# Projection stage of an encoder trunk: two weight sums a group and the first heads' biases from VectorE to GpSimd, a fourth raw weight buffer, and the stores that keep x spread over the first stage

## The chip, the core and the metric

The kernel runs on one core of a Trainium2 chip. The core has a matrix engine (PE, called TensorE), VectorE (DVE), ScalarE (ACT), GpSimd (POOL) and a queue engine (SP), each with its own in-order queue of instructions; they meet only through semaphores. 16 DMA engines move data between HBM and the on-chip memory (SBUF); transfers are issued from SP, ACT or POOL. PE writes its results into PSUM banks. The metric is the device time of one execution in microseconds (us), the median of several runs.

## What is computed

Two layers of an encoder over 512 tokens of width 1024, all in float32. Cut to what matters here:

```
h = h + 0.5 * post(SwiGLU(pre(h)))            # feed-forward 1
u = pre(h);  proj = u @ w_in[l]               # 54 column blocks of 128
qa, ka, va, qb, kb, vb, qc, kc, vc, gates = split(proj)
A: neighbourhood attention, bias = rpb looked up by relative place, plus a mask
B: sliding-window attention     C: differential attention
h = h + post((sum_i gate_i * (branch_i @ W_branch_i)) @ W_out)
h = h + 0.5 * post(SwiGLU(pre(h)))            # feed-forward 2
```

Every matrix product is made with three matmuls: each operand is divided into a high part (a rounded copy, by ACT) and a low part (the rest, by DVE), and high*high, high*low and low*high are summed.

## The kernel before, in words

**Stages.** Each layer runs feed-forward 1 ("f"), the projections ("p", `project`), attention and mixing ("m", `mixer`) and feed-forward 2. In the profiled execution the projections of layer 0 lie at about 346 to 512 us and those of layer 1 at 1510 to 1668 us.

**Groups by Strassen.** In "f" and "p" most products run in groups of two column blocks with seven half-sized products instead of eight (class `Seven`, a variant of Strassen's method). One group is 84 matmuls of 128x256 on PE. "p" has 13 groups a layer, numbered g = 0 to 12 (`GROUPS`), after a few blocks that are made in the ordinary way (`COVER`). For each group DVE and ACT make the weights ready while PE works on the group before: two raw blocks of 512 KB are fetched (`fetches`, line L206), then come `sum13` (DVE, L628, 128x1024), `high1`/`low1` (ACT L632, DVE L637), `high13`/`low13` (ACT L642, DVE L647), `sum2` (DVE, L651, 128x512: writes the quarter s2 into the second raw block), `high12`/`low12` (ACT L657, DVE L661), `sum4` (DVE, L665, 128x512: after low12 has read that quarter) and `high24`/`low24` (ACT L669, DVE L674). DVE also closes each group's sums (`add21` L740, `add22` L745, which read PSUM) and, in "p", makes low parts of results (L1413), rotary products (L1459 to L1461) and transposed values (L1441, which read PSUM).

**Raw weights.** All raw blocks go through three buffers "wr", turn by turn. A fetch waits until the block that lay in its buffer has been read for the last time. So the second fetch of group g+2 goes into the buffer that holds the first block of group g+1.

**GpSimd.** In "p" POOL only issues stores of finished pieces to HBM (`store`, L1407). Each waits in POOL's queue until ACT or DVE has written its piece. In "f" it makes a one-column copy ("mark", L287) ahead of each of its transfers.

**Tiles.** Pieces of 128x512 in "p" come from a ring of 16 buffers "t"; a buffer comes free when its store has landed.

**Biases.** `mixer` adds masks to the looked-up table in four additions a head (`put`, L1750). For heads 0 and 1 the inputs are loaded in "p" (`tables_of_a`, called in group 6 of the program text, moved forward by the scheduler) and the additions run in "p" as well; for the other heads they run in "m".

**First stage.** At the start x lies transposed in SBUF. `keep(tb)` (L905 to L912) turns it back by 2 x 4 transposes of PE into the only bank "o", ACT copies each bank into a tile "h" of a ring of 4 (shared with the tiles t and v of the same stage), and SP stores it to HBM. Four `keep` calls give 8 such rounds. They are entries of a list `later`: small pieces of work that are taken up two at a time whenever a new weight tile is fetched. Ten more entries follow them (differences of the operand's quadrants and their high and low parts, and the first group's weights).

**What sets the order.** Outside two regions with an order by hand, a scheduler that lays out the whole program ahead of time decides the order on each engine's queue; on the chip each queue is then strictly in order.

Of the kernel before, what the change touches and what calls it, by code (L numbers as in the profile page):

```python
# [21 lines left out]
NT = T // P  # L22
FF = 2816
KF = FF // P
# [4 lines left out]
WB = 8  # L29
# [85 lines left out]
def encoder_kernel(ctx: ExitStack, tc: tile.TileContext, order, xT, wts, cols, rows, rpb, consts, tables, out):  # L115
    nc = tc.nc
# [8 lines left out]
    BUFS = {"X": 6, "n": 2, "wr": 3, "wp": 2, "wq": 2}  # L125
    WP = BUFS["wp"] + BUFS["wq"]
    SKEW = 80
    ABUFS = {"f": {"t": 4, "x": 10}, "p": {"t": 16, "x": 10, "rr": 2}, "m": {"t": 5, "h": 4, "rr": 2, "tx": 5, "st": 14, "gd": 2, "g": 10, "s": 2, "pt": 4}}
    PBUFS = {"mm": 2, "mx": 2, "at": 3, "o": 1}

    def open_phase(kind):
# [10 lines left out]
    def nm(s):  # L142
        serial[0] += 1
        return f"{s}{serial[0]}"
# [53 lines left out]
    def holder(tag):  # L198
        return lambda: [big(tag, F32R, (P, HB, P), name="w") for _ in range(2)]

    def fetch(parts, eng=None):
        raw = sb.tile([P, WB, P], F32, tag="wr", name=nm("wr"), bufs=BUFS["wr"])
        src = wts[len(stream["raw"])].rearrange("p (a b) -> p a b", b=P)
        for c in range(0, WB, WB // parts):
            cs = slice(c, c + WB // parts)
            (eng or stream["eng"]).dma_start(raw[:, cs, :], src[:, cs, :])  # L206
        stream["raw"].append(raw)
# [167 lines left out]
    class Squares:  # L375
        def __init__(self):
            self.acc, self.seen = None, []
# [203 lines left out]
    class Seven:  # L581


        def __init__(self, z, count):
            self.z, self.count = z, count
# [28 lines left out]
        def fetches(self, g):  # L614
            if g < self.count:
                self.W[g] = {}
                for _ in range(2):
                    fetch(1, nc.sync)
# [29 lines left out]

        def sum2(self, g):
            r = self.raws[g]  # L650
            V.tensor_tensor(out=r[1][:, 1], in0=self.W[g]["r13"][:, 1], in1=r[0][:, 0], op=ALU.add)  # L651

        def high12(self, g):
            w = self.W[g]
# [7 lines left out]

        def sum4(self, g):
            r = self.raws[g][1]
            V.tensor_tensor(out=r[:, 0], in0=r[:, 0], in1=r[:, 1], op=ALU.add)  # L665

        def high24(self, g):
            self.W[g]["h24"] = self.wpair("h24")
# [96 lines left out]
    def ffn(l, which, X, accs):  # L765
# [93 lines left out]
                V.scalar_tensor_tensor(out=place(m), in0=pu, scalar=-1.0, in1=t, op0=ALU.mult, op1=ALU.mult)  # L859


        S = Seven(z, KF - plain)
# [7 lines left out]
        def at(fn, *args):  # L870
            return lambda: fn(*args)
# [13 lines left out]
        if first:  # L885
# [33 lines left out]
            later.extend(at(keep, tb) for tb in range(NT))  # L919
            later.append(at(gap, "gaph", 48))  # L920
        else:
            quadrants(X.raw)
# [14 lines left out]
                at(S.low1, 0),  # L937
            )
        )
        if not first:  # L940
            u1 = dense1(gu, l, KF + 1, X.blocks, tag="at")
        finish(0, g0, u0)
# [427 lines left out]
    def project(l, op, accs):  # L1370
# [115 lines left out]
            now()  # L1486

        made = {}
        S = Seven(z, len(GROUPS))
        count, groups, later = S.count, S.groups, stream["later"]  # L1490

        def some(*calls):
# [226 lines left out]
    def mixer(l, op, made):  # L1719
# [15 lines left out]
        def biases(hd):  # L1735
# [10 lines left out]
            def put(dst, mask, n0, n1):  # L1746

                src = raw[:, 7 * RPBW + 39 - 8 * n0 :]
                (ps0, pn), _ = src.ap
                V.tensor_tensor(  # L1750
                    out=dst.rearrange("p (d r c) -> p d r c", r=8, c=8),
                    in0=bass.AP(src.tensor, src.offset, [[ps0, pn], [-8, n1 - n0], [-RPBW, 8], [-1, 8]]),
                    in1=mask.rearrange("p (d r c) -> p d r c", r=8, c=8),
                    op=ALU.add,
                )
# [402 lines left out]
```

## Time and profile before

| what | value |
|---|---|
| median of 3 runs | 2344.84 us (2342.85 to 2346.62) |
| profiled execution | 2345.54 us, its span 2343.7 us |
| PE busy | 2329.0 us (99% of the span) |
| DVE busy | 1917.7 us (82%) |
| ACT busy | 1455.2 us (62%) |
| POOL busy | 235.7 us (10%) |
| granted TensorE clock | 0.999 |

The span runs from the first to the last instruction; the execution's own time is 1.8 us more. "Busy" of PE is the union of its matmul records, whose ends are modelled; so what matters here is the time in which PE is not busy at all, 14.7 us of the span, and in which stage that lies.

### The profile page before, as it was taken

Reading aid. Unit: us, or ns where it says so; the run is one execution under the profiler, and the core shown is the slowest. Engines: PE = TensorE matmul, PEld = TensorE weight load, DVE = VectorE, ACT = ScalarE, POOL = GpSimd, SP = SyncE. Lnnn points to the kernel's source line nnn. Section 1 sums busy time; section 2 is a strip of 40 time slices with the busy share of each in tenths; the row PEclk is TensorE's granted clock in tenths of the full one; section 3 lists DMA queues with packets and bytes.
Section 4 is the critical chain, followed back from the end, with each engine's and each line's share of the span. In section 5 each row is a group of like instructions: output and inputs, shape, how many; then the busy total and the mean of one; then the engine's idle time right before and its main releaser. Section 6 shows DMA issues by size and latency. Waiting matters only on the chain.

```text
span 2343.7 us, 40580 instructions
## 1 busy us (share of the span) xinstructions
PE 2329.0 (99%) x15278; PEld 2104.4 (90%) x15278; DVE 1917.7 (82%) x3103; ACT 1455.2 (62%) x2734; POOL 235.7 (10%) x378
## 2 busy tenths in 40 slices
PE   9999999999999999999999999999999999999998
PEld 7999889998888889998899998899988888999987
DVE  8987988868987778888888878798689776888796
ACT  6565566668766465655665555666687764656563
POOL 0111001110122001110001100011102110011100
PEclk9999999999999999999999999999999999999999
DMA  5566446668556425665536565276775664356642
GB/s 190 148 172 194 147 150 194 200 218 241 150 179 214 149 96 151 168 160 161 171 103 165 166 171 197 92 219 197 231 221 147 187 207 142 97 162 171 180 142 92
DMA packets 135636, 395.18 MB, mean 169 GB/s; under 512 B 19216, under 2 KB 23952, under 8 KB 134928
## 3 DMA queue, kind: packets, MB, share of 16 engines
q1 hardware_dynamic: 99712, 260.11, 35.8%
q0 software_dynamic: 22080, 84.95, 13.3%
q10 hardware_dynamic: 13648, 47.53, 6.6%
q8 instruction: 120, 1.97, 0.4%
q14 instruction: 76, 0.62, 0.1%
HBM read 326.98 MB, written 80.74 MB: 174 GB/s over the span
## 4 chain that ended last, share of the span: by engine, by line
PE 88%; DMA 4%; DVE 3%; issue 2%; ACT 1%; SPq 0%; POOL 0%; ACTq 0%; DVEq 0%; POOLq 0%
PE mm L687 20%; PE mx L687 10%; PE mm L1155 8%; PE mm L323 6%; PE mm L322 6%; PE mm L324 6%; PE mx L1155 5%; PE at L687 5%; PE at L1155 5%; DMA wr<-in_wts_dram 2%; PE at L322 2%; PE at L323 2%; PE at L324 2%; PE o L1155 1%; PE mx L1677 1%
## 5 line engine op out<-in xcount | busy, mean ns | idle before, releaser
L687 PE MATMUL mm<-X,h 128*128 128x256 f32 x1600 | 285.5, 278 | 2.3 <-DVE v L745 2.2
L687 PEld LDWEIGHTS mm<-X,h 128*128 128x128 f32 x1600 | 243.1, 188 | 4.3 <-DVE v L745 3.4
L687 PE MATMUL mm<-ht,h 128*128 128x256 f32 x800 | 224.0, 280 | 1.0 <-ACT at L726 1.0
L687 PE MATMUL mm<-ht,l 128*128 128x256 f32 x800 | 223.6, 279 | 0.0
L687 PE MATMUL mm<-lt,h 128*128 128x256 f32 x800 | 222.8, 278 | 0.0
L687 PE MATMUL mx<-ht,h 128*128 128x256 f32 x800 | 221.6, 277 | 0.4 <-ACT v L731 0.2
L687 PE MATMUL mm<-X,l 128*128 128x256 f32 x800 | 221.5, 277 | 0.0
L687 PE MATMUL mx<-ht,l 128*128 128x256 f32 x800 | 221.2, 276 | 0.0
L687 PE MATMUL mx<-lt,h 128*128 128x256 f32 x800 | 221.2, 276 | 0.0
L219 ACT ACTIVATE w<-wr 128x512 fp32r<-128x512 f32 x240 | 148.1, 626 | 96.4 <-PE mm L324 54.7
L220 DVE TENSOR_TENSOR w<-wr,w 128x512 fp32r<-128x512 f32 x240 | 163.0, 687 | 49.6 <-ACT w L219 48.6
L322 PE MATMUL mm<-X,w 128*128 128x512 f32 (+1 forms) x516 | 196.3, 380 | 0.3 <-ACT w L219 0.3
L323 PE MATMUL mm<-X,w 128*128 128x512 f32 (+1 forms) x516 | 195.4, 379 | 0.2
L324 PE MATMUL mm<-X,w 128*128 128x512 f32 (+1 forms) x516 | 193.6, 375 | 0.0
L637 DVE TENSOR_TENSOR l<-wr,h 128x1024 fp32r<-128x1024 f32 x100 | 122.4, 1224 | 67.8 <-PE mm L687 67.6
L669 ACT ACTIVATE h<-wr 128x1024 fp32r<-128x1024 f32 x100 | 106.2, 1062 | 84.1 <-PE mx L687 56.1
L687 PE MATMUL at<-X,w 128*128 128x256 f32 x1200 | 153.7, 277 | 0.0
L687 PEld LDWEIGHTS mm<-ht,h 128*128 128x128 f32 x800 | 150.7, 188 | 1.6 <-ACT at L726 1.4
L687 PEld LDWEIGHTS mx<-ht,h 128*128 128x128 f32 x800 | 150.3, 188 | 1.1 <-ACT v L731 1.0
L687 PEld LDWEIGHTS mm<-ht,l 128*128 128x128 f32 x800 | 150.8, 188 | 0.3 <-DVE l L674 0.2
L687 PEld LDWEIGHTS mm<-lt,h 128*128 128x128 f32 x800 | 150.7, 188 | 0.0
L687 PEld LDWEIGHTS mx<-lt,h 128*128 128x128 f32 x800 | 150.3, 188 | 0.0
(462 smaller groups left out, 6767.0 us busy)
## 6 DMA issues: line engine op xcount, KB each, us to landing
wr<-in_wts_dram SPq DMA_DIRECT2D x284, 512.0 KB, 3.7
wr<-in_wts_dram ACTq DMA_DIRECT2D x90, 512.0 KB, 4.2
sum<-in_wts_dram POOLq DMA_DIRECT2D x64, 512.0 KB, 5.1
st<-part SPq DMA_DIRECT2D x120, 128.0 KB, 4.2
ap<-in_wts_dram SPq DMA_DIRECT2D x20, 512.0 KB, 6.0
a<-kept SPq DMA_DIRECT2D x32, 256.0 KB, 6.3
ap<-sum SPq DMA_DIRECT2D x16, 512.0 KB, 3.3
x<-part SPq DMA_DIRECT2D x32, 256.0 KB, 3.6
```

The costliest lines, as they stand in the source:

```text
L219: A.activation(hi, raw, AF.Copy)
L220: V.tensor_tensor(out=lo, in0=raw, in1=f(hi), op=ALU.subtract)
L322: PE.matmul(acc, w[0], x[0], start=start, stop=False)
L323: PE.matmul(acc, w[0], x[1], start=False, stop=False)
L324: PE.matmul(acc, w[1], x[0], start=False, stop=stop)
L637: V.tensor_tensor(out=w["l1"], in0=self.raws[g][0], in1=f(w["h1"]), op=ALU.subtract)
L669: A.activation(self.W[g]["h24"], self.raws[g][1], AF.Copy)
L687: PE.matmul(acc, ws[i], xs[j], start=start and k == m == 0, stop=stop and k == n - 1 and m == 2, skip_group_check=True,)
L1155: PE.matmul(acc, x[i], w[j], start=start and n == 0, stop=stop and n == 2, skip_group_check=True)
L1677: PE.matmul(shaped(sp, k), qs, k, start=m == 0, stop=m == 1)
```

## The change

Four edits, three of them in "p":

- `sum2` and `sum4` of groups 2 to 12 are issued on GpSimd (`self.adder`), those of groups 0 and 1 stay on VectorE; the class is also used in "f", where the adder stays VectorE. That is 22 additions of 128x512 a layer.
- The four `put` additions of heads 0 and 1 are issued on GpSimd: 8 a layer, four of 128x256 and four of 128x128.
- In "p" the second raw block of every odd group goes to a buffer of its own, "wx". So there are four raw buffers for two groups, and a fetch for group g+2 waits for group g alone. The room comes from the ring "t", which has 14 buffers now.
- The four `keep` entries are no longer in one row ahead of the other ten: they stand before the first, second, third and fourth of these.

```
--- before.py
+++ after.py
@@ -125,7 +125,7 @@
     BUFS = {"X": 6, "n": 2, "wr": 3, "wp": 2, "wq": 2}
     WP = BUFS["wp"] + BUFS["wq"]
     SKEW = 80
-    ABUFS = {"f": {"t": 4, "x": 10}, "p": {"t": 16, "x": 10, "rr": 2}, "m": {"t": 5, "h": 4, "rr": 2, "tx": 5, "st": 14, "gd": 2, "g": 10, "s": 2, "pt": 4}}
+    ABUFS = {"f": {"t": 4, "x": 10}, "p": {"t": 14, "x": 10, "rr": 2}, "m": {"t": 5, "h": 4, "rr": 2, "tx": 5, "st": 14, "gd": 2, "g": 10, "s": 2, "pt": 4}}
     PBUFS = {"mm": 2, "mx": 2, "at": 3, "o": 1}
 
     def open_phase(kind):
@@ -198,8 +198,9 @@
     def holder(tag):
         return lambda: [big(tag, F32R, (P, HB, P), name="w") for _ in range(2)]
 
-    def fetch(parts, eng=None):
-        raw = sb.tile([P, WB, P], F32, tag="wr", name=nm("wr"), bufs=BUFS["wr"])
+    def fetch(parts, eng=None, raw=None):
+        if raw is None:
+            raw = sb.tile([P, WB, P], F32, tag="wr", name=nm("wr"), bufs=BUFS["wr"])
         src = wts[len(stream["raw"])].rearrange("p (a b) -> p a b", b=P)
         for c in range(0, WB, WB // parts):
             cs = slice(c, c + WB // parts)
@@ -581,8 +582,8 @@
     class Seven:
 
 
-        def __init__(self, z, count):
-            self.z, self.count = z, count
+        def __init__(self, z, count, adder):
+            self.z, self.count, self.adder = z, count, adder
             self.hi, self.lo, self.raw = {}, {}, {}
             self.raws, self.W = {}, {}
             self.groups = [{} for _ in range(count)]
@@ -614,8 +615,9 @@
         def fetches(self, g):
             if g < self.count:
                 self.W[g] = {}
-                for _ in range(2):
-                    fetch(1, nc.sync)
+                for i in range(2):
+                    own = phase[0][0] == "p" and i and g % 2
+                    fetch(1, nc.sync, self.z("wx", F32, (P, WB, P)) if own else None)
                 self.raws[g] = [t.rearrange("p (a b) c -> p a b c", a=2) for t in stream["raw"][-2:]]
 
         def wpair(self, name):
@@ -648,7 +650,7 @@
 
         def sum2(self, g):
             r = self.raws[g]
-            V.tensor_tensor(out=r[1][:, 1], in0=self.W[g]["r13"][:, 1], in1=r[0][:, 0], op=ALU.add)
+            (self.adder if g > 1 else V).tensor_tensor(out=r[1][:, 1], in0=self.W[g]["r13"][:, 1], in1=r[0][:, 0], op=ALU.add)
 
         def high12(self, g):
             w = self.W[g]
@@ -662,7 +664,7 @@
 
         def sum4(self, g):
             r = self.raws[g][1]
-            V.tensor_tensor(out=r[:, 0], in0=r[:, 0], in1=r[:, 1], op=ALU.add)
+            (self.adder if g > 1 else V).tensor_tensor(out=r[:, 0], in0=r[:, 0], in1=r[:, 1], op=ALU.add)
 
         def high24(self, g):
             self.W[g]["h24"] = self.wpair("h24")
@@ -859,7 +861,7 @@
                 V.scalar_tensor_tensor(out=place(m), in0=pu, scalar=-1.0, in1=t, op0=ALU.mult, op1=ALU.mult)
 
 
-        S = Seven(z, KF - plain)
+        S = Seven(z, KF - plain, V)
         hi, lo, raw, groups, count = S.hi, S.lo, S.raw, S.groups, S.count
         divide, less, quadrants = S.divide, S.less, S.quadrants
         later = stream["later"]
@@ -916,7 +918,6 @@
                 later.append(some(at(normal, b), at(normal, b + 1)))
             later.append(at(divide, "11", own[0][:, 0], own[1][:, 0]))
             later.append(at(divide, "22", own[0][:, 1], own[1][:, 1]))
-            later.extend(at(keep, tb) for tb in range(NT))
             later.append(at(gap, "gaph", 48))
         else:
             quadrants(X.raw)
@@ -937,6 +938,9 @@
                 at(S.low1, 0),
             )
         )
+        if first:
+            for tb in range(NT):
+                later.insert(len(later) - 10 + tb, at(keep, tb))
         if not first:
             u1 = dense1(gu, l, KF + 1, X.blocks, tag="at")
         finish(0, g0, u0)
@@ -1486,7 +1490,7 @@
             now()
 
         made = {}
-        S = Seven(z, len(GROUPS))
+        S = Seven(z, len(GROUPS), G)
         count, groups, later = S.count, S.groups, stream["later"]
 
         def some(*calls):
@@ -1747,7 +1751,7 @@
 
                 src = raw[:, 7 * RPBW + 39 - 8 * n0 :]
                 (ps0, pn), _ = src.ap
-                V.tensor_tensor(
+                (G if hd < 2 else V).tensor_tensor(
                     out=dst.rearrange("p (d r c) -> p d r c", r=8, c=8),
                     in0=bass.AP(src.tensor, src.offset, [[ps0, pn], [-8, n1 - n0], [-RPBW, 8], [-1, 8]]),
                     in1=mask.rearrange("p (d r c) -> p d r c", r=8, c=8),
```

**DVE, layer 0, group 7 of "p" while the weights of group 8 (r_5254, wr_5206 and wr_5208) are made ready.** Before:

```order
L628 TENSOR_TENSOR r_5254<-wr_5208,wr_5206 128x1024
L661 TENSOR_TENSOR w_5290<-wr_5208,w_5290 128x512
L637 TENSOR_TENSOR l_5270<-wr_5206,h_5251 128x1024
L651 TENSOR_TENSOR wr_5208<-r_5254,wr_5206 128x512
L647 TENSOR_TENSOR l_5307<-r_5254,h_5268 128x1024
L740 TENSOR_TENSOR v_5272<-mx_5235,v_5272 128x256
L665 TENSOR_TENSOR wr_5208<-wr_5208 128x512
L1413 TENSOR_TENSOR lo_5360<-x_4931,hi_5359 128x512
L745 TENSOR_TENSOR v_5272<-mm_5234,v_5272 128x256
L674 TENSOR_TENSOR l_5382<-wr_5208,h_5355 128x1024
```

and now (line numbers are two higher in this part, L1413 is L1417):

```order
L630 TENSOR_TENSOR r_5254<-wx_5208,wr_5206 128x1024
L742 TENSOR_TENSOR v_5139<-mx_5102,v_5139 128x256
L1465 TENSOR_TENSOR v_4862<-v_4862,sh_5018 128x512
L676 TENSOR_TENSOR l_5249<-wr_5069,h_5222 128x1024
L1417 TENSOR_TENSOR lo_5226<-v_4725,hi_5225 128x512
L747 TENSOR_TENSOR v_5139<-mm_5101,v_5139 128x256
L663 TENSOR_TENSOR w_5290<-wx_5208,w_5290 128x512
L630 TENSOR_TENSOR r_5387<-wr_5341,wr_5339 128x1024
L639 TENSOR_TENSOR l_5270<-wr_5206,h_5251 128x1024
L649 TENSOR_TENSOR l_5307<-r_5254,h_5268 128x1024
L742 TENSOR_TENSOR v_5272<-mx_5235,v_5272 128x256
L676 TENSOR_TENSOR l_5382<-wx_5208,h_5355 128x1024
```

`sum2` and `sum4` are gone from DVE's queue, and `sum13` of a group now stands ahead of the closing sums v_5139 and of the low part l_5249 of the group before, where it stood behind them; even sum13 of the group after (r_5387) stands ahead of low1 (l_5270).

**POOL, layer 0, the start of the groups** (edges and pre are the biases' outputs and inputs, wr_4224 and r_4263 belong to group 2). Now:

```order
L1411 DMA part_4099<-v_4092 128x512
L1754 ISA
L1754 TENSOR_TENSOR edges_5100<-pre_5095 128x256
L653 TENSOR_TENSOR wr_4224<-r_4263,wr_4222 128x512
L1754 TENSOR_TENSOR edges_5100<-pre_5095 128x128 x2
L1754 TENSOR_TENSOR edges_5100<-pre_5095 128x256 x2
L1754 TENSOR_TENSOR edges_5100<-pre_5095 128x128
L667 TENSOR_TENSOR wr_4224<-wr_4224 128x512
L1411 DMA part_4301<-hi_4297 128x512
L1411 DMA part_4303<-lo_4298 128x512
L653 TENSOR_TENSOR wx_4365<-r_4409,wr_4363 128x512
```

Before, the store of part_4301 came right behind that of part_4099. The row "ISA" reloads POOL's library of routines; it stands there once, and not in layer 1. Between the two sums of group 2 stand bias additions (one more of 128x256 is left out here), and between later sums stand stores that wait for ACT and DVE.

**ACT, the copies h of the first stage** (o is the bank, h the tile of the ring of 4 that is stored). Before:

```order
L910 ACTIVATE h_471<-o_466 128x512
L206 DMA wr_611<-in_wts_dram 128x1024
L854 ACTIVATE t_486<-t_486 128x512
L910 ACTIVATE h_504<-o_499 128x512
L219 ACTIVATE w_564<-wr_562 128x512
L910 ACTIVATE h_512<-o_507 128x512
L600 ACTIVATE ht_567<-n_358 128x1024
L910 ACTIVATE h_521<-o_516 128x512
```

and now:

```order
L912 ACTIVATE h_455<-o_450 128x512
L601 ACTIVATE X_359<-n_358 128x1024
L220 ACTIVATE w_512<-wr_477 128x512
L207 DMA wr_611<-in_wts_dram 128x1024
L856 ACTIVATE t_470<-t_470 128x512
L912 ACTIVATE h_489<-o_484 128x512
L220 ACTIVATE w_551<-wr_549 128x512
L601 ACTIVATE ht_515<-n_358 128x1024
L912 ACTIVATE h_497<-o_492 128x512
```

Before, four copies had been made by h_471 and a further two follow the tiles t and v of the ring; now two copies stand ahead of t and v (h_455 is the second), and the next two come with more work between them.

More of the change, by code (lines that the diff above doesn't have):

```diff
@@ L127, in encoder_kernel @@
     SKEW = 80
-    ABUFS = {"f": {"t": 4, "x": 10}, "p": {"t": 16, "x": 10, "rr": 2}, "m": {"t": 5, "h": 4, "rr": 2, "tx": 5, "st": 14, "gd": 2, "g": 10, "s": 2, "pt": 4}}
+    ABUFS = {"f": {"t": 4, "x": 10}, "p": {"t": 14, "x": 10, "rr": 2}, "m": {"t": 5, "h": 4, "rr": 2, "tx": 5, "st": 14, "gd": 2, "g": 10, "s": 2, "pt": 4}}
     PBUFS = {"mm": 2, "mx": 2, "at": 3, "o": 1}
@@ L199, in holder, with fetch @@
         return lambda: [big(tag, F32R, (P, HB, P), name="w") for _ in range(2)]
-    def fetch(parts, eng=None):
-        raw = sb.tile([P, WB, P], F32, tag="wr", name=nm("wr"), bufs=BUFS["wr"])
+    def fetch(parts, eng=None, raw=None):
+        if raw is None:
+            raw = sb.tile([P, WB, P], F32, tag="wr", name=nm("wr"), bufs=BUFS["wr"])
         src = wts[len(stream["raw"])].rearrange("p (a b) -> p a b", b=P)
@@ L581, in encoder_kernel, with __init__ @@
     class Seven:
-        def __init__(self, z, count):
-            self.z, self.count = z, count
+        def __init__(self, z, count, adder):
+            self.z, self.count, self.adder = z, count, adder
             self.hi, self.lo, self.raw = {}, {}, {}
@@ L616, in fetches @@
                 self.W[g] = {}
-                for _ in range(2):
-                    fetch(1, nc.sync)
+                for i in range(2):
+                    own = phase[0][0] == "p" and i and g % 2
+                    fetch(1, nc.sync, self.z("wx", F32, (P, WB, P)) if own else None)
                 self.raws[g] = [t.rearrange("p (a b) c -> p a b c", a=2) for t in stream["raw"][-2:]]
@@ L650, in sum2 @@
             r = self.raws[g]
-            V.tensor_tensor(out=r[1][:, 1], in0=self.W[g]["r13"][:, 1], in1=r[0][:, 0], op=ALU.add)
+            (self.adder if g > 1 else V).tensor_tensor(out=r[1][:, 1], in0=self.W[g]["r13"][:, 1], in1=r[0][:, 0], op=ALU.add)
         def high12(self, g):
@@ L664, in sum4 @@
             r = self.raws[g][1]
-            V.tensor_tensor(out=r[:, 0], in0=r[:, 0], in1=r[:, 1], op=ALU.add)
+            (self.adder if g > 1 else V).tensor_tensor(out=r[:, 0], in0=r[:, 0], in1=r[:, 1], op=ALU.add)
         def high24(self, g):
@@ L859, in finish @@
                 V.scalar_tensor_tensor(out=place(m), in0=pu, scalar=-1.0, in1=t, op0=ALU.mult, op1=ALU.mult)
-        S = Seven(z, KF - plain)
+        S = Seven(z, KF - plain, V)
         hi, lo, raw, groups, count = S.hi, S.lo, S.raw, S.groups, S.count
@@ L918, in ffn @@
             later.append(at(divide, "22", own[0][:, 1], own[1][:, 1]))
-            later.extend(at(keep, tb) for tb in range(NT))
             later.append(at(gap, "gaph", 48))
@@ L939, in ffn @@
         )
+        if first:
+            for tb in range(NT):
+                later.insert(len(later) - 10 + tb, at(keep, tb))
         if not first:
@@ L1488, in project @@
         made = {}
-        S = Seven(z, len(GROUPS))
+        S = Seven(z, len(GROUPS), G)
         count, groups, later = S.count, S.groups, stream["later"]
@@ L1749, in put @@
                 (ps0, pn), _ = src.ap
-                V.tensor_tensor(
+                (G if hd < 2 else V).tensor_tensor(
                     out=dst.rearrange("p (d r c) -> p d r c", r=8, c=8),
```

## The prediction

> **What bounds the kernel now.** I read first where PE, the busiest engine, is not busy, stage by stage, in the view of busy time by stretch (length; then busy us and instruction count of PE, weight loads, DVE, ACT, POOL; clock; DMA share; GB/s).
>
> ```profile
> 0.00:72.00 72.00, 69.09 (x337) 57.84 (x337) 59.94 (x106) 46.34 (x78) 2.14 (x8) 1.00 0.51 169
> 72.00:223.00 151.00, 151.00 (x1321) 150.81 (x1321) 128.64 (x163) 87.65 (x145) 24.87 (x30) 1.00 0.62 167
> 346.00:512.00 166.00, 164.27 (x1339) 159.80 (x1338) 140.45 (x196) 106.69 (x199) 24.85 (x46) 1.00 0.62 196
> 1510.00:1668.00 158.00, 156.00 (x1255) 150.81 (x1254) 136.38 (x187) 100.97 (x188) 22.73 (x42) 1.00 0.64 198
> 2214.00:2343.70 129.70, 123.50 (x597) 102.81 (x595) 97.56 (x113) 64.71 (x92) 0.00 (x0) 0.99 0.41 133
> ```
>
> PE is the bound. The change adds and removes no matmul, so it can win only the time in which PE waits where the change works: part of 2.91 us in the first stage, 1.73 us in the projections of layer 0 and 2.00 us in those of layer 1. The 6.2 us at the end are out of its reach. What it can lose has no such bound: where DVE's work in the projections gets longer than PE's, DVE becomes the clock. So I read next who made PE wait, in the view of waits cut to three stretches: 36 to 62 us (one row), 391 to 502 (three) and 1552 to 1665 (two); us, times, longest.
>
> ```profile
> PE o L908 <- ACT h L910: 1.6, 1, 1.6
> ...
> PE at L1434 <- DVE v L1441: 0.8, 1, 0.8
> PE mm L687 <- DVE v L745: 0.7, 2, 0.5
> PE mx L687 <- ACT v L731: 0.2, 1, 0.2
> ...
> PE mm L687 <- ACT at L726: 1.0, 1, 1.0
> PE mm L687 <- DVE v L745: 0.6, 2, 0.4
> ```
>
> These are few and short waits. In the projections most are for DVE, which was late with a sum or a transposed value.
>
> **The stores of x (first stage).** One wait of 1.6 us. Its cause is ahead of ACT:
>
> ```profile
> 49.53 0.60 ACT L910 ACTIVATE h<-o 128x512 f32<-128x512 f32 x1 [2.78 <-DMA kept<-h]
> DMA to landing us min/median/max: 2.0/4.0/5.6
> ```
>
> The first row is ACT's timeline, the second the landing times of the eight stores at L911. The sixth copy waited 2.78 us for its tile h, since a store from the ring of four had not landed, and PE's next transposes waited for the one bank. In the new order a copy's tile was last used by tiles t and v, which have no store, or by a store with at least 23 matmuls and two other copies in between, where before four copies stood in a row and the sixth met the fourth's store. I take it that even a store of 5.6 us has landed by then. What it can cost: three of the four last rounds stand close together, and a copy of 0.60 us may show between them. So the bounds are -1.6 and +0.6 us; I take **-1.3 us**, near the wait that is seen, since its cause is removed and the spacing of the later rounds is like that of the early rounds of before, which did not wait.
>
> **What leaves DVE.** The two rows of the sums in the groups by line between 391 and 502 us, with the rows that read PSUM, and the bias additions of the whole run (ns, min/median/max):
>
> ```profile
> L665 DVE TENSOR_TENSOR wr<-wr 128x512 f32<-128x512 f32 x11 | 7.6, 687 | 0.1
> L651 DVE TENSOR_TENSOR wr<-r,wr 128x512 f32<-128x512 f32 x11 | 7.5, 684 | 0.0
> L740 DVE TENSOR_TENSOR v<-mx,v 128x256 f32<-128x256 f32 x11 | 4.6, 421 | 0.9 <-PE mx L687 0.9
> L745 DVE TENSOR_TENSOR v<-mm,v 128x256 f32<-128x256 f32 x11 | 4.6, 419 | 0.0
> L1441 DVE TENSOR_TENSOR v<-at,v 128x256 fp32r<-128x256 f32 x6 | 2.5, 420 | 0.0
> L1750 DVE TENSOR_TENSOR edges<-pre x16: 282/353/421, 390.2 to 1575.6; 128x256 f32<-128x256 f32 x8, 128x128 f32<-128x128 f32 x8
> ```
>
> ```profile
> 391.00:502.00 111.00, 109.27 (x942) 108.18 (x941) 99.62 (x138) 72.79 (x139) 20.46 (x38) 1.00 0.65 207
> 1552.00:1665.00 113.00, 111.04 (x947) 109.46 (x947) 100.26 (x139) 73.56 (x140) 20.48 (x38) 1.00 0.64 204
> ```
>
> Sums 7.6 + 7.5 = 15.1 us and eight additions of 0.35 us = 2.8 us a layer leave DVE: 99.6 becomes about 81.7 of 111 us, and 100.3 becomes 82.4 of 113.
>
> **What it costs on POOL.** The trace has no addition on POOL. Below, a sum costs what DVE takes for it, 0.69 us. Above, I add POOL's dearest small instruction, the one-column copy:
>
> ```profile
> L287 POOL COPY mark<-a x53: 757/1046/1047, 93.9 to 2199.5; 128x1 f32<-128x1 f32 x53
> 93.66 1.22 DVE L647 TENSOR_TENSOR l<-r,h 128x1024 fp32r<-128x1024 f32 x1
> 93.88 1.03 POOL L287 COPY mark<-a 128x1 f32<-128x1 f32 x1 [8.12 <-DVE a L982]
> 94.79 0.42 DVE L740 TENSOR_TENSOR v<-mx,v 128x256 f32<-128x256 f32 x1
> ```
>
> 1.05 + 0.69 = 1.74 us. I take the middle, 1.2 us, and for a bias addition the share of its size (256 or 128 of 512 columns, on average 0.375), 0.45 us. That is 22 x 1.2 + 8 x 0.45 = 30 us a layer. POOL was busy 20.5 of 111 us, so the work fits in its queue.
>
> The rows show something else. A copy of one column that lasts 1.03 us and ends at 94.91 does not work that long: L647, which reads two SBUF operands, ends at 94.88. So POOL got at its operand when DVE's instruction let go. I assume the same the other way: while POOL adds, a DVE instruction with two SBUF operands waits. DVE's idle time (111 - 81.7 = 29.3 us) and the rows that read PSUM (4.6 + 4.6 + 2.5 = 11.7 us) are free of that; the other 70 us, 63% of the stretch, are not. If POOL's 30 us fall without regard to DVE, 0.63 x 30 = 19 us are added to DVE: 81.7 + 19 = 101 of 111 us, against 99.6 before. **So I count no relief of DVE at all.** With 0.69 us a sum it would be 92.6 us, with 1.74 us for a sum and 1.4 us for a bias 113 us.
>
> [...]
>
> **The fourth raw buffer.** What DVE and ACT waited for between 391 and 502 us (two rows), DVE between 1552 and 1665 (one), and what the fetches in SP's queue waited for between 391 and 502 (last):
>
> ```profile
> DVE r L628 <- DMA wr<-in_wts_dram: 4.8, 8, 0.9
> ...
> ACT w L657 <- DMA wr<-in_wts_dram: 9.5, 8, 3.2
> ...
> DVE r L628 <- DMA wr<-in_wts_dram: 2.7, 5, 1.2
> ...
> SPq L206 <- DVE l L637: 26.5, 5, 7.4
> ```
>
> DVE stood still 4.8 and 2.7 us for raw blocks that came late, and the fetches were late because the buffer still held the first block of the next group until low1 (L637) had read it. With "wx" a fetch no longer waits for that, and the new order has sum13 a third of a group earlier. Those stops of DVE go, and with them some of PE's waits behind them (the closing sum L745 stands in the order close to L628). The earlier sum13 also covers the longer way of the two sums over POOL. All of PE's waits in both stages are 1.73 + 2.00 = 3.7 us; one of 1.0 us is ACT's, and the others need not all come from the raw blocks. I take half, **-1.9 us**; the bounds are -3.7 and the rivals below.
>
> **The smaller ring "t".** No cost: a store lands 4.5 us (at most 6.5) after its issue in the view by line, and 14 buffers are two groups of work. If POOL's queue delays stores, that cover shrinks.
>
> ```profile
> DMA to landing us min/median/max: 2.2/4.5/6.5
> ```
>
> **Sum.** -1.3 - 1.9 = -3.2 us on the profiled execution of 2345.54 us (span 2343.7 and 1.8 us around it): 2342.3. That execution lies 0.7 us above the median of the runs, 2344.84, so the prediction is **2341.6 us** for the median, -0.14%. A change below 0.2%, 4.7 us, can hardly be told from none for this kernel.
>
> **Rivals.**
>
> *All waits go.* The exclusion touches little, since POOL's sums come early and find gaps. Then -1.6 - 3.7 = -5.3 us: 2339.5. For it: DVE's queue is 18 us shorter in each stage. Against: one of PE's longest waits there is ACT's.
>
> *POOL's queue is late at the first groups.* In layer 0 POOL reloads its library and makes seven bias additions ahead of sum4 of group 2. POOL's row before:
>
> ```profile
> 384.69 0.54 POOL L1407 DMA_DIRECT2D part<-v  x1 [1.53 <-DVE v L1441]
> 395.81 0.54 POOL L1407 DMA_DIRECT2D part<-hi  x1 [10.58 <-ACT v L735]
> 398.42 0.68 DVE L665 TENSOR_TENSOR wr<-wr 128x512 f32<-128x512 f32 x1
> ```
>
> POOL is free from 385.2 us; before, sum4 of group 2 ended on DVE at 399.1, 13.9 us later. Two sums and seven additions are 5.6 us, and if each of the nine waits half of a DVE instruction of 1.22 us, 5.5 us more: 11.1 us. A reload over 2.8 us makes sum4 late, and DVE's low24, the sums behind it and PE with it. The stores of the next pieces then queue behind it as well. [...]
>
> *DVE becomes the bound.* Slower: a sum holds the port for 1.4 us, and nearly every one lands on a DVE instruction with two SBUF operands, since these are queued without gaps. Then DVE needs 81.7 + 22 x 1.4 + 8 x 0.525 = 116.7 of 111 us and 82.4 + 35 = 117.4 of 113: +5.7 + 4.4 - 1.3 = +8.8, 2353.6. It decides from 81.7 + 25 p = 111, a price p of 1.17 us that is wholly on top. Against it: 41 us of DVE's time there are free of the exclusion.
>
> **How the numbers follow.** Forecast 47% (own range 2340 to 2344), all waits go 20%, POOL late at the start 17%, DVE the bound 16%. Faster by over 0.2% (under 2340.2): the second case and a little of the first, 0.24. Slower by over 0.2% (over 2349.5): the last case and the dear end of the third, 0.18. Within: 0.58. The range reaches from 2337.5, two us under the second case for waits that the records do not show as idle time, to 2350, where the last case begins: it leaves out about 2 in 10.
>
> **What would show it.** In the new profile: the wait of PE for h (L912) is gone from the first 72 us; DVE's waits for "wr" or "wx" are gone; PE's idle time between 391 and 502 us is near 0.9 us instead of 1.73; POOL's additions last about 1.2 us, or up to 1.2 us longer when they start beside a DVE addition, and DVE's additions beside them have longer records or start late. I am wrong if DVE's busy time in that stretch comes out well under 95 us (then the exclusion is small), if it fills the stretch and PE's waits for DVE grow, or if PE shows a new wait of some us near 400 us.

## The result

The changed kernel takes 2382.11 us (2376.48 to 2387.12), the kernel before 2344.84 us: the ratio is 1.0158 [1.0146, 1.0171], 37 us slower. The profiled execution has a span of 2380.5 us against 2343.7, 36.8 us more. Two single executions among the experiments, 4704.5 us with the fourth buffer and 3876.7 us with `sum2` alone on POOL, lie far outside the rest and are left out of the ratios and of the second kernel's median (the first one's, 2347.74, would be 2347.47).

Busy time by stretch of the kernel after (length; busy us and count of PE, weight loads, DVE, ACT, POOL; clock; DMA share; GB/s), then the first row of its page:

```profile
0.00:72.00 72.00, 70.18 (x353) 59.19 (x354) 61.79 (x109) 47.16 (x80) 2.14 (x8) 1.00 0.54 177
391.00:502.00 111.00, 97.30 (x776) 95.94 (x775) 85.14 (x95) 62.86 (x119) 56.50 (x60) 0.92 0.54 176
```

```profile
PE 2339.8 (98%) x15278; PEld 2114.9 (89%) x15278; DVE 1911.4 (80%) x3043; ACT 1458.8 (61%) x2734; POOL 322.9 (14%) x438
```

The first stage gained: PE is busy 1.1 us more in the first 72 us. The loss is in the projections. Between 391 and 502 us PE stands 13.7 us where it stood 1.7, and it did not meet its old pace while it ran: the granted clock is 0.92. Over the whole span PE's idle time is 2380.5 - 2339.8 = 40.7 us against 14.7 (+26.0), and its busy time grew by 10.8 us although it runs the same 15278 matmuls. Here are the stretches in which the clock was granted by half, one after each of PE's longest stalls:

```profile
403.59:410.41 6.82, 4.79 (x22) 4.79 (x23) 5.17 (x7) 4.32 (x10) 4.01 (x6) 0.50 0.69 240
451.37:458.20 6.83, 6.23 (x29) 6.23 (x30) 6.44 (x9) 1.67 (x4) 0.00 (x0) 0.50 0.18 52
...
sum 30.71, PE 24.61 PEld 24.62 DVE 24.15 ACT 16.79 POOL 12.43; mean PE 4.10 PEld 4.10 DVE 4.02 ACT 2.80 POOL 2.07
```

The sum goes over six such stretches, three in each layer; the kernel before has none in its projections.

Who made PE wait (whole span; us, times, longest), and what DVE waited for at `sum13` (now L630) between 391 and 502 us:

```profile
PE mm L689 <- DVE v L747: 17.4, 8, 4.7
PE at L1438 <- DVE lo L1417: 7.6, 2, 4.1
```

```profile
DVE r L630 <- DMA wx<-in_wts_dram: 11.4, 3, 4.6
DVE r L630 <- issue: 5.1, 2, 2.6
...
DVE r L630 <- DMA wr<-in_wts_dram: 2.1, 2, 1.7
```

PE waits for DVE's closing sums (L747) and low parts (L1417). DVE does not fill the stretch: it is busy for 85.1 us of 111 and gets through 95 instructions where it made 138. It is late: 18.6 us of the stretch it stands at `sum13` for a raw block, against 4.8 before, with all that is queued behind. ("issue" is a wait without a releaser in the records; both times `sum13` reads a pair "wr" that was fetched shortly before.)

The exclusion between the two engines can be seen directly. DVE and POOL in layer 0, then lines of the whole run (ns, min/median/max):

```profile
442.64 1.23 DVE L630 TENSOR_TENSOR r<-wx,wr 128x1024 f32<-128x1024 f32 x1 [4.57 <-DMA wx<-in_wts_dram]
443.78 1.22 DVE L639 TENSOR_TENSOR l<-wr,h 128x1024 fp32r<-128x1024 f32 x1
443.95 2.21 POOL L653 TENSOR_TENSOR wx<-r,wr 128x512 f32<-128x512 f32 x1 [4.77 <-DVE r L630]
444.92 2.32 DVE L649 TENSOR_TENSOR l<-r,h 128x1024 fp32r<-128x1024 f32 x1
447.16 0.41 DVE L742 TENSOR_TENSOR v<-mx,v 128x256 f32<-128x256 f32 x1
```

```profile
L667 POOL TENSOR_TENSOR wx<-wx x10: 1277/1295/1578, 407.2 to 1676.4; 128x512 f32<-128x512 f32 x10
L1754 POOL TENSOR_TENSOR edges<-pre x16: 446/1290/1717, 387.1 to 1577.2; 128x256 f32<-128x256 f32 x8, 128x128 f32<-128x128 f32 x8
L649 DVE TENSOR_TENSOR l<-r,h x100: 1211/1220/2322, 63.4 to 2245.7; 128x1024 fp32r<-128x1024 f32 x100
L747 DVE TENSOR_TENSOR v<-mm,v x100: 408/418/425, 75.5 to 2257.7; 128x256 f32<-128x256 f32 x100
```

`sum2` is released by the end of `sum13` (L630) and begins beside L639, which reads two SBUF operands. It lasts 2.21 us, 0.93 longer than the 1.28 of an undisturbed sum, until about when L639 lets go plus 1.28. L649, begun at 444.92, lasts 1.1 us too long and ends 1.1 us after the sum. Here they take turns, each for a whole instruction. L747, which reads PSUM and one SBUF operand, is never lengthened (at most 425 ns in 100).

### The profile page after: what moved, and what is told of

It is laid out like the page before. It is cut to its first block, busy times and chain, and to the rows that moved or that the text cites. A ratio compares the mean times of both kernels' runs of the same rounds, so it can differ in the third digit from the quotient of the medians.

```text
span 2380.5 us, 40656 instructions
## 1 busy us (share of the span) xinstructions
PE 2339.8 (98%) x15278; PEld 2114.9 (89%) x15278; DVE 1911.4 (80%) x3043; ACT 1458.8 (61%) x2734; POOL 322.9 (14%) x438
## 5 line engine op out<-in xcount | busy, mean ns | idle before, releaser
L689 PE MATMUL mm<-X,h 128*128 128x256 f32 x1600 | 292.0, 282 | 17.4 <-DVE v L747 17.4
L689 PEld LDWEIGHTS mm<-X,h 128*128 128x128 f32 x1600 | 247.9, 192 | 20.0 <-DVE v L747 19.4
L639 DVE TENSOR_TENSOR l<-wr,h 128x1024 fp32r<-128x1024 f32 x100 | 123.4, 1234 | 73.4 <-PE mm L689 73.4
L689 PEld LDWEIGHTS mm<-X,l 128*128 128x128 f32 x800 | 153.3, 192 | 0.0
```

What stands on the lines that cost most here:

```text
L639: V.tensor_tensor(out=w["l1"], in0=self.raws[g][0], in1=f(w["h1"]), op=ALU.subtract)
L689: PE.matmul(acc, ws[i], xs[j], start=start and k == m == 0, stop=stop and k == n - 1 and m == 2, skip_group_check=True,)
```

## The experiments

The theories, as the expectations name them. **A**: DVE and POOL shut each other out of SBUF while POOL adds. **B**: the bias additions in POOL's queue make the sums late. **C**: the raw buffer, the ring and the order that came with them cost. **D**: the way over POOL makes the ring "load, sum13, sum2, sum4, low24, next load" longer, and DVE stands at `sum13`. Line numbers shift by a few where an experiment adds lines: `sum13` is L630 or L634.

The parts of the change together. The three columns at the right are read in 391 to 502 us: PE busy, DVE busy and DVE's waits for raw blocks at `sum13`. A slower kernel does less of its work in that stretch.

| kernel | us | ratio to before | PE | DVE | waits |
|---|---|---|---|---|---|
| before | 2344.84 | | 109.3 | 99.6 | 4.8 |
| stores of x alone | 2343.61 | 0.9992 [0.9983, 1.0001] | 109.8 | 100.2 | 2.6 |
| + fourth raw buffer, ring 14 | 2347.74 | 1.0012 [1.0002, 1.0022] | 107.9 | 98.1 | 8.7 |
| + buffer, biases on POOL | 2350.64 | 1.0025 [1.0016, 1.0033] | 105.5 | 96.4 | 11.7 |
| + buffer, sums on POOL | 2371.21 | 1.0108 [1.0094, 1.0122] | 98.9 | 87.9 | 16.8 |
| all (the change) | 2382.11 | 1.0158 [1.0146, 1.0171] | 97.3 | 85.1 | 18.6 |

### The change in parts

The first run is the kernel before with this alone:

```
-            later.extend(at(keep, tb) for tb in range(NT))
...
+        if first:
+            for tb in range(NT):
+                later.insert(len(later) - 10 + tb, at(keep, tb))
```

> The kernel before with the one edit of the stores that keep x. All theories of the loss are about the projections, so all expect the 1.6 us wait of PE for h in the first stage to go and nothing else to move: -1.3 us against before (bounds -1.6 and +0.6), about 2343.5 us, PE busy about 70.2 of the first 72 us instead of 69.1. A loss of more than 1 us would say that some of the 37 us come from here.

It measured 2343.61 us, 1.2 less than the runs of before beside it (2344.77), though the interval touches 1. As forecast.

The others start from the change and take parts back:

```
-        S = Seven(z, len(GROUPS), G)
+        S = Seven(z, len(GROUPS), V)
...
-                (G if hd < 2 else V).tensor_tensor(
+                V.tensor_tensor(
```

Both hunks together leave the stores and the fourth buffer:

> The changed kernel with the sums and the bias additions back on VectorE: what stays is the moved stores of x, the fourth raw buffer and the ring t of 14. Theory A (VectorE and GpSimd keep each other from SBUF while GpSimd adds) and theory B (GpSimd's queue: the sums stand behind bias additions and come late) both expect no loss: 2341 to 2344 us, VectorE's waits for the raw blocks (4.8 and 2.7 us in the two layers) gone, the granted clock 1.0 throughout. Theory C (the loss comes from the buffer, the smaller ring or the order of the block loads that these bring) expects PE stalls of 3 to 5 us in the projections and at least 2355 us.

2347.74 us: 4.1 us slower than the stores alone. No theory had this: not the 2355 us or more of C, and not the gain of A, B and of the prediction. DVE's waits for raw blocks did not go. Its waits and its order in this kernel:

```profile
DVE r L630 <- DMA wx<-in_wts_dram: 5.9, 3, 3.4
DVE r L630 <- DMA wr<-in_wts_dram: 2.8, 2, 2.0
```

```profile
428.05 1.22 DVE L676 TENSOR_TENSOR l<-wx,h 128x1024 fp32r<-128x1024 f32 x1
429.19 0.69 DVE L663 TENSOR_TENSOR w<-wr,w 128x512 fp32r<-128x512 f32 x1
429.79 0.42 DVE L747 TENSOR_TENSOR v<-mm,v 128x256 f32<-128x256 f32 x1
430.12 0.68 DVE L667 TENSOR_TENSOR wr<-wr 128x512 f32<-128x512 f32 x1
434.23 1.23 DVE L630 TENSOR_TENSOR r<-wx,wr 128x1024 f32<-128x1024 f32 x1 [3.42 <-DMA wx<-in_wts_dram]
```

```profile
429.29 0.33 SPq L207 DMA_DIRECT2D wx<-in_wts_dram  x1
```

L676, `low24` of group 5, is the last reader of "wx". 20 ns after its end the fetch for group 7 is issued, and `sum13` of group 7 (L630) stands only three short instructions later in DVE's queue. The load takes till 434.2. So the buffer still binds, and the new order puts `sum13` ahead of work that could have filled the time. This order is not the sums' doing: without the sums' own rows, DVE's order here differs from that of the change in a few places only.

The sums alone and the biases alone, one hunk each:

> The changed kernel with only the bias additions back on VectorE; the 22 sums a layer stay on GpSimd. Theory B expects the first and longest stall of each layer (4.8 us at 400.7, 4.7 us at 1582.2) to go, with its stretch of half clock (6.8 us, worth 3.4): 8.2 us a layer, so about 2382 - 16 = 2366 us or less, and if the later stalls are its aftermath, near 2345. Theory A expects the later stalls (448.8, 492.0, 1629.8, 1671.8) to stay as they are and the first to shrink only by the queueing: 2366 to 2382 us, with VectorE instructions of 2 us and more beside GpSimd's sums.

> The changed kernel with the sums back on VectorE; only the eight bias additions of the first two heads in each layer are on GpSimd. Theory A expects little: 8 x 1.3 = 10 us of GpSimd a layer against VectorE, once, near the start of the stage: 0 to +3 us on the result of the kernel with the sums and the biases both on VectorE, no stall at 448 or 1630 us. Theory B without the sums behind the additions expects no loss either, since then only the edges themselves are late: 2341 to 2345 us. A loss of 8 us or more would say that the bias additions alone make VectorE late, whatever the sums do.

2371.21 and 2350.64 us. The sums cost 23.5 us on top of 2347.74, the biases 2.9 (the two intervals in the table overlap), and together they cost 34.4, 8.0 more than one by one. The early stall of PE, 4.7 us up to 405.6 in the change, is 1.9 us up to 401.5 with the sums alone; the later ones, near 445 and 487 us in this run, stay. So the sums are where A had them and B had not, the biases alone are in A's range of 0 to +3 and not where B had them, and B may hold for the 8 us. The whole: -1.2 + 4.1 + 23.5 + 2.9 + 8.0 = 37.3 us.

### Reads without a chain, and a chain without reads

From here on the biases are on VectorE unless the text says otherwise. First, 22 additions a layer whose results nobody waits for, beside sums on VectorE (the ring t has 13 buffers here, for the room of the tile that they write):

```
+        def beside(self, g, a, b):
+            if phase[0][0] == "p" and g > 1:
+                G.tensor_tensor(out=self.dm, in0=a, in1=b, op=ALU.add)
...
             V.tensor_tensor(out=r[1][:, 1], ...)
+            self.beside(g, r[1][:, 1], r[1][:, 1])
...
             V.tensor_tensor(out=r[:, 0], ...)
+            self.beside(g, r[:, 0], r[:, 1])
```

> The kernel with moved stores, fourth raw buffer and sums and biases on VectorE (2347.7 us), and beside it 22 additions of 128x512 a layer on GpSimd that read two finished blocks and write a tile that nobody reads (ring t 13 for its room): GpSimd's reads without VectorE, ScalarE or PE waiting for their results. VectorE's and PE's order is the same as without them. Theory A (VectorE and GpSimd shut each other out of SBUF) expects most of the 23.5 us that the sums on GpSimd cost: at least +12, 2360 us or more, with VectorE instructions of over 2 us beside them. Theory D (the way over GpSimd makes the ring load - sum13 - sum2 - sum4 - low24 - next load longer, VectorE stands at sum13 for the raw block, and what is behind it is late) expects at most +4: 2347 to 2352 us.

2375.77 us, ratio 1.0126 [1.0109, 1.0143]: 28.0 us of loss from additions whose results are not used. DVE's order is that of the row "+ fourth raw buffer, ring 14" of the table. The first rows of the pages of that run, of the sums on POOL, and of this one:

```profile
PE 2326.5 (99%) x15278; PEld 2103.0 (90%) x15278; DVE 1915.5 (82%) x3103; ACT 1458.6 (62%) x2734; POOL 236.2 (10%) x378
```

```profile
PE 2334.9 (99%) x15278; PEld 2110.2 (89%) x15278; DVE 1915.0 (81%) x3059; ACT 1458.7 (62%) x2734; POOL 314.4 (13%) x422
```

```profile
PE 2337.2 (98%) x15278; PEld 2111.3 (89%) x15278; DVE 1945.3 (82%) x3103; ACT 1457.3 (61%) x2734; POOL 315.7 (13%) x422
```

44 additions made the same 3103 DVE instructions longer by 29.8 us, 14.9 a layer. With the real sums on POOL, DVE lost 44 sums (44 x 0.686 = 30.2 us) and its busy time is 1915.0 against 1915.5: what left came back as holds. In 391 to 502 us DVE is busy 100.5 and waits 7.1 at `sum13`, 107.6 of 111, while PE did 97.4 us of work: here DVE is the clock. (The reads also hold blocks a little longer, but the waits at `sum13` are not above the 8.7 us of the kernel without them.) But DVE still makes the 44 sums here, so the holds come on top of a full queue, where in the change they take the place of the sums. The run shows that reads alone can cost this much, not how the 23.5 us come about.

The counterpart keeps the chain and takes away the reads; each sum on POOL is replaced by two writes, so the sums of groups 2 to 12 are left out of the output:

```
+        def write(self, t):
+            for _ in range(2):
+                G.memset(t, 0.01)
```

> The kernel with the sums on GpSimd and the biases on VectorE (2371.2 us), where each of the 44 sums is two writes of a constant into the same place: same waits and the same order of VectorE and PE, but GpSimd reads nothing (the output leaves out these sums). Theory D expects the loss to stay if a pair of writes lasts about as long as an addition (1.3 us): 2363 to 2373 us, VectorE's waits at sum13 still over 14 us a layer. Theory A expects the result of the sums on VectorE: 2345 to 2352 us.

2346.56 us, ratio 1.0004 [0.9994, 1.0013]. Its groups by line (first row), waits and stretch:

```profile
L628 POOL MEMSET wr<- 128x512 f32 x48 | 25.4, 530 | 51.5 <-DVE r L634 32.0 <-DMA wr<-in_wts_dram 13.7 <-DVE w L667 4.8
```

```profile
DVE r L634 <- DMA wx<-in_wts_dram: 10.1, 3, 4.3
DVE r L634 <- issue: 4.6, 2, 2.3
DVE r L634 <- DMA wr<-in_wts_dram: 3.5, 2, 1.9
```

```profile
391.00:502.00 111.00, 109.64 (x948) 108.83 (x948) 84.32 (x116) 73.04 (x139) 42.19 (x80) 1.00 0.63 209
```

A pair of writes is 1.06 us, 0.2 less than an addition, in the same place of the same order. DVE waits 18.2 us at `sum13`, as much as in the change, and PE loses nothing: DVE is relieved (84.3 us), comes early, and waits in time it has to spare. So D alone is refuted as the cause, and the waits at `sum13` alone are no loss. Without POOL's reads, taking the sums from DVE would have cost nothing, and gained nothing that shows: the 1.2 us below 2347.74 are within the noise. The writes are neither held off (530 and 532 ns on average, 48 and 40 of them) nor do they hold DVE (`low1`, 100 of 128x1024, lasts 1223 ns on average here as in the run without sums on POOL, and 1241 ns beside the 44 reads); how the 23.5 us divide between these two sides of the exclusion no run separates.

So in this pair of runs DVE and POOL were in each other's way where POOL read SBUF (28.0 us, DVE's instructions 29.8 us longer) and not where it only wrote (-1.2 us). VectorE's side, which the trace of before could not show, is in L649 (up to 2.32 us for 1.22) and L747 (at most 425 ns) above.

### More raw buffers, fewer sums

A fifth buffer, first with the sums on POOL, then with all on VectorE (the edit is the same, ring t 12):

```
-                    fetch(1, nc.sync, self.z("wx", F32, (P, WB, P)) if own else None)
+                    fetch(1, nc.sync, self.z(f"wx{g // 2 % 2}", F32, (P, WB, P)) if own else None)
```

> The kernel with the sums on GpSimd and the biases on VectorE (2371.2 us), with a fifth raw buffer: the second blocks of the odd groups take turns in two buffers, ring t 12. Theory D expects the loads for the odd groups' second blocks to come a whole group pair earlier, VectorE's wait at sum13 (16.5 and 16.8 us a layer) to fall by more than half, and the time by 10 us or more: 2350 to 2361 us. Theory A expects 2366 to 2372 us, since GpSimd reads as much as before.

> The kernel with sums and biases on VectorE (2347.7 us) with the same fifth raw buffer and ring t 12: the cost of the smaller ring without the sums. If the 4 us that the fourth buffer lost against the kernel with the moved stores alone (2343.6) are VectorE's waits for the raw block at sum13 (8.7 us in 391 to 502), they go: 2341 to 2345 us. If the smaller ring t costs, it is 2348 us or more.

2361.32 us, ratio 1.0066 [1.0051, 1.0081], and 2341.58 us, ratio 0.9984 [0.9974, 0.9993]. The waits for a load at `sum13` fell from 16.8 to 7.9 us and from 8.7 to 3.4:

```profile
DVE r L630 <- DMA wr<-in_wts_dram: 3.4, 3, 1.4
```

With them went 9.9 us beside the sums on POOL, and 6.2 us with the sums on VectorE. Read with the run of writes, this says that the waits at `sum13` count where DVE has little time to spare. The sums' own cost hardly went with them: between these two kernels it is 19.7 us, where it was 23.5. The second of these kernels is faster than both the kernel before and the change (3.3 us less than before; against the stores alone, 2343.61 in another run, the 2 us are not settled). It needs none of GpSimd's additions.

Another division of five buffers, three for all first blocks and two for all second ones, sums on VectorE:

```
-                    own = phase[0][0] == "p" and i and g % 2
+                    own = phase[0][0] == "p" and i
...
+                    fetch(1, nc.sync, self.z(f"wx{g % 2}", F32, (P, WB, P)) if own else None)
```

> The kernel with moved stores, sums and biases on VectorE and five raw buffers (2341.6 us when the second blocks of the odd groups have two), now with three buffers for the first blocks and two for the second blocks of all groups. If VectorE's waits for raw blocks are all that the fifth buffer took away, it is the same within 2 us: 2340 to 2344 us. If a buffer's turn still decides, the even division shows less waiting at sum13 (3.4 us in 391 to 502 with the other division) and 2338 to 2341 us.

2348.30 us, ratio 1.0016 [1.0007, 1.0025], with 9.6 us of waits at `sum13`, all for "wx". Neither expectation held. So the number of buffers alone does not decide; that it is how early the next one comes free fits the waits, but no run tests it by itself.

Three buffers, as before, with the sums on POOL (`own = False`, ring t 16):

> The kernel with the sums on GpSimd and the biases on VectorE (2371.2 us) without the fourth raw buffer, ring t 16: the moved stores and the sums alone, in an order of VectorE that is nearly that of the kernel before. If the sums cost the same 23.5 us wherever the buffers are, it is 2343.6 + 23.5 = 2367 us. If the order that came with the fourth buffer (sum13 ahead of the low parts that free the buffer) is a partner in the loss, VectorE waits for raw blocks well under 16.5 us in 391 to 502, and it is 2350 to 2360 us. If the fourth buffer took waits away from the sums, as the prediction had it, it is 2372 us or more with longer waits at sum13.

2361.02 us, ratio 1.0059 [1.0042, 1.0076], 17.4 us over the stores alone; a microsecond above the range for a partner. So the fourth buffer costs 10.2 us beside sums on POOL and 4.1 without them, but the sums by themselves, with 2.6 us of waits at `sum13`, cost 17.4: with three, four and five buffers 17.4, 23.5 and 19.7 us. Where these come from is seen in POOL, DVE and ACT of this kernel:

```profile
403.24 4.94 POOL L653 TENSOR_TENSOR wr<-r,wr 128x512 f32<-128x512 f32 x1 [0.26 <-DVE r L630]
...
406.95 0.41 DVE L742 TENSOR_TENSOR v<-mx,v 128x256 f32<-128x256 f32 x1
408.26 1.29 POOL L667 TENSOR_TENSOR wr<-wr 128x512 f32<-128x512 f32 x1
...
409.58 1.06 ACT L671 ACTIVATE h<-wr 128x1024 fp32r<-128x1024 f32 x1 [3.33 <-POOL wr L667]
...
410.68 1.23 DVE L676 TENSOR_TENSOR l<-wr,h 128x1024 fp32r<-128x1024 f32 x1 [3.31 <-ACT h L671]
```

This is the exclusion from the other side: DVE's instructions with two SBUF operands followed each other without a gap until L742, which reads PSUM, and `sum2` took 4.94 us. `sum4`, high24 on ACT and low24 on DVE came late one after the other, DVE stood 3.31 us, and PE 1.85 us behind it.

Half of the sums:

```
-            (self.adder if g > 1 else V).tensor_tensor(out=r[:, 0], in0=r[:, 0], in1=r[:, 1], op=ALU.add)
+            V.tensor_tensor(out=r[:, 0], in0=r[:, 0], in1=r[:, 1], op=ALU.add)
```

and the same with sum2 in place of sum4.

> The kernel with the sums on GpSimd and the biases on VectorE (2371.2 us), with sum4 back on VectorE: only sum2 on GpSimd, released by the end of sum13, so that it always starts on VectorE's next instructions. Theory A says that every hold on the burst of VectorE's work behind a late sum13 is paid: with half the holds, 8 to 14 us of the 23.5 stay: 2356 to 2362 us. If the loss has a threshold (VectorE full only with all of them), it is 2348 to 2354 us.

> The same with sum2 back on VectorE: only sum4 on GpSimd, which follows low12 and is followed by ScalarE's high24 and VectorE's low24. Theory A: 2356 to 2362 us, as with sum2 alone. If it is the longer way to low24, which frees the raw block, that costs, sum4 alone costs more than sum2 alone: 2362 us or more against 2354 or less.

2365.86 us, ratio 1.0094 [1.0075, 1.0112], and 2364.81 us, 1.0083 [1.0070, 1.0097]: 18.1 and 17.1 us over 2347.74. Both miss A's range and that of a threshold, and `sum4` alone is not dearer than `sum2` alone, as the longer way to low24 would have it: half of the sums cost nearly what all cost. With sum4 alone on POOL one sum in each layer took 7.43 us:

```profile
L667 POOL TENSOR_TENSOR wr<-wr x12: 1287/1460/7432, 392.5 to 1671.4; 128x512 f32<-128x512 f32 x12
```

Part of it is that the other sum is again DVE's. DVE's busy time, less the sums that left it, grew by 21.2 us with `sum2` on POOL (1921.6 us in all), 10.0 with `sum4` (1910.4) and 29.7 with both (1915.0): the holds add up, the time does not. Why it saturates so early is not settled: the clock is at half for 10.2 us in each of the two kernels and for 17.1 us with all sums, and DVE's orders differ a little; no run separates these.

The queue of POOL at the start of the groups, in the change with its biases on POOL:

```
-            (self.adder if g > 1 else V).tensor_tensor(
+            (self.adder if g > 3 else V).tensor_tensor(
```

(in both sums)

> The changed kernel with the sums of groups 2 and 3 back on VectorE; the sums of groups 4 to 12 and the eight bias additions a layer stay on GpSimd. Theory B (the bias additions stand in GpSimd's queue ahead of sum4 of group 2, so the first stall of a layer comes) expects the stalls at 400.7 and 1582 us (4.8 and 4.7 us) and the half clock behind them to go: the sums' 23.5 us by 18/22 are 19.2, and with the biases' own 2.9 us on 2347.7 it is 2369.8: 2366 to 2373 us. If the biases and the sums add up to 34.4 us for another reason (GpSimd's reads alone), 4 sums fewer are worth some 5 us: 2375 to 2379 us.

2370.73 us, ratio 1.0109 [1.0095, 1.0122], as B had it. What went is this, POOL and DVE in the change:

```profile
390.09 1.29 POOL L653 TENSOR_TENSOR wr<-r,wr 128x512 f32<-128x512 f32 x1 [1.69 <-DMA pre<-in_rpb_dram]
391.34 8.20 POOL L1754 TENSOR_TENSOR edges<-pre 128x256 f32<-128x256 f32 x6
399.51 1.28 POOL L667 TENSOR_TENSOR wr<-wr 128x512 f32<-128x512 f32 x1
```

```profile
401.91 2.72 DVE L676 TENSOR_TENSOR l<-wr,h 128x1024 fp32r<-128x1024 f32 x1 [2.35 <-ACT h L671]
404.56 0.68 DVE L1417 TENSOR_TENSOR lo<-x,hi 128x512 fp32r<-128x512 f32 x1
405.16 0.41 DVE L747 TENSOR_TENSOR v<-mm,v 128x256 f32<-128x256 f32 x1
```

Between sum2 and sum4 of group 2 stand 8.2 us of bias additions; sum4 ends at 400.8, low24 (L676) begins at 401.9 and lasts 2.72 us beside POOL's next sum (402.3 to 403.5), and the closing sum for which PE waited 4.7 us ends at 405.6. With the first sums on DVE, PE's waits for DVE between 391 and 412 us are 1.1 us instead of 5.4, and the clock is at half in the projections for 17.1 us instead of 30.7.

## Why the prediction was wrong

**The stores of x**, -1.3: measured -1.2 us, with an interval that just reaches no gain, and PE's wait for L912 is gone.

**What leaves DVE** and **what it costs on POOL**. The price of a sum, 1.2 us, was close: 1.28 where nothing is in the way. A bias addition was put at 0.45 us by its size and takes 1.29 in the median, since most meet DVE (the six that last 8.20 us from 391.34 us run beside DVE's L676, L663, L639, L649, L1417 and L630, which follow each other without a gap from 390.39 to 399.22 us); a 128x128 one with no instruction of DVE beside it (400.75 us) takes 0.45. "So I count no relief of DVE at all": right over the whole run, 1915.0 against 1915.5 us with the sums alone, by 14.9 us of holds a layer where the step had 19. That it comes out to half a microsecond is luck: a sum is worth 0.69 us on DVE and its holds happen to cost 0.68 on average.

**The first step that failed is what was made of this.** DVE's 101 of 111 us was taken to cost nothing. The holds do not fall "without regard to DVE": `sum2` is released by `sum13`, so it starts beside the two-operand instructions that are queued right behind, and L747, on which PE waits, is at their end. And POOL's share was left out: a sum held off by DVE (4.94 - 1.28 = 3.7 us in the row above) makes high24 and low24 late. Reads on top of DVE's own sums cost 28.0 us, the sums with three buffers 17.4, where the step had zero; that writes in the same places, without reads, cost nothing puts this on the exclusion. The trace of before had two pieces of it, VectorE shutting out GpSimd in L287's row (1.03 us for one column, ending 0.03 us after L647) and the queue in DVE's order.

**The second is the fourth raw buffer**: "Those stops of DVE go", -1.9. They grew from 4.8 to 8.7 us with the sums on DVE (+4.1 us) and to 18.6 in the change; with the sums on POOL the fourth buffer costs 10 us against three. I read the earlier `sum13` in the new order as cover for the sums; it put DVE in front of a load that low24, three instructions earlier, had only just let start. Moving `sum4` away also took one of the few instructions that stood in that gap; that this matters is argued from the order alone.

**The ring t** of 14, no cost: not tested alone; with 12 buffers and five raw blocks the kernel with all sums on VectorE was the fastest of all, so no cost of it shows.

**The rivals.** "DVE becomes the bound" had the holds and their direction, with a price of 8.8 us; its 1.4 us a sum was my assumption, and 1.28 was measured where nothing is in the way. It had no waits at `sum13` and no clock in it. "POOL's queue is late at the first groups" named the 400 us stall with the right links. It comes in both layers and is worth 8.0 us beyond the two parts. The reload that this rival took for its cause is not what showed: POOL's first addition waits 4.64 us for its input anyway, until 387.14 us, and layer 1 has no reload. The reload's own two records (MODIFY_POOL_CONFIG) last 37 ns each at 382.5 us; that it takes longer than these no run shows. "All waits go" was as far off as could be: no wait went but the first stage's.

**No term at all** stood for the clock: PE's busy time grew by 10.8 us. By the sum row above PE was busy for 24.6 us at half clock, which would be some 12.3 us at the full one, an estimate that is near this.

## What to carry to other kernels

Before an elementwise add goes from VectorE to GpSimd, list what VectorE runs beside it: if these are instructions with two SBUF operands, both engines can pay, as they did here (on VectorE 2.32 us for 1.22, on GpSimd 2.21 to 4.94 us for 1.28 in the rows above), and the price was set here by what stands behind the held instruction, not by VectorE's share of busy time. When a buffer is added to let loads start earlier, look where the last reader of the old block and the first reader of the new one stand in the same engine's queue; the time between them must hold a load. And a stall of a few microseconds on PE costs more than its length where the granted clock drops behind it, as it did in the change for 30.7 us in six stretches.

## What the runs showed of the hardware that was not expected

- **PE's clock.** In these runs it was granted by half for 3.41 or 6.83 us after some stalls of PE; in the change it was 30.7 us in all within the projections. The length of the stall does not decide it. One of 1.85 us was followed by half the clock with three buffers and the sums on POOL (first two rows, stretches of that kernel), and one as long was not when the fourth buffer was there as well (last two rows):

```profile
411.50:414.91 3.41, 1.56 (x14) 1.36 (x13) 3.41 (x6) 3.11 (x7) 1.99 (x3) 1.00 0.75 239
414.92:418.33 3.41, 3.41 (x19) 3.41 (x18) 2.44 (x3) 1.63 (x7) 1.59 (x2) 0.50 0.46 183
```

```profile
396.78:400.20 3.42, 2.82 (x25) 2.62 (x23) 3.42 (x5) 2.81 (x5) 2.35 (x2) 1.00 0.64 249
400.20:403.61 3.41, 2.16 (x18) 2.16 (x19) 3.41 (x6) 1.80 (x5) 2.82 (x5) 1.00 0.92 308
```

The columns are those of the views by stretch above. In every run the changes of the clock lie whole windows of 3.41 us apart (in the change 1, 2, 11, 12, 117, 204 or 318 of them). The first stall lies within one such window (PE idle for 1.85 of 3.41 us), the second is cut by the border of two (0.60 and 1.25 us). Take the windows at the full clock of all fifteen kernels, from 20 us on: each of the 44 with PE idle for more than 1.9 us was followed by half the clock. Of those with less only three were, with 1.85, 1.85 and 1.56 us idle, while two with 1.87 and 1.85 us were not, so in these runs the border is near 1.9 us, a little over half a window, but not sharp. In the profiled executions of before and of the change alone, the eight windows with 2.13 to 3.41 us idle were followed by half the clock and none with 1.68 us or less was.

- **The exclusion works both ways and can starve GpSimd.** A DVE instruction of 1.22 us took up to 2.72, and an addition of 1.28 us on GpSimd 4.94 (three buffers), 7.43 (`sum4` alone) and, beside sums on VectorE, 2.00 and 1.59 us on average (24 on "wr", 20 on "wx"). Writes alone (0.53 us for 128x512) met none of it.
